# Five scheduling edits around the end of a recurrence: interleaving rate, page pool, load order, integer positions, gate rank

## The chip, the cores and the metric

The kernel runs on one core of one Trainium2 chip, as a single launch. The metric is the device time of that launch in microseconds; lower is better. A core has five engines with a queue of instructions each: TensorE (PE; its weight loads are shown as PEld), VectorE (DVE), ScalarE (ACT), GpSimd (POOL), and SyncE (SP), which here only issues transfers. An engine takes its instructions in the order in which they were written down at compile time and waits on semaphores for the others. SBUF is on-chip memory, PSUM the accumulator banks of PE, DRAM the memory outside.

## The reference

One layer over 1024 tokens of width 1024, cut to what the change touches:

```python
h = adaln(x, shift1, scale1)
p = h @ w_in                                  # conv columns and recurrence columns
y_conv = silu(layer_norm(causal_conv31(glu(p_conv))))
y_rw = rwkv7(p_rw)                            # state recurrence over the 1024 tokens, 8 heads of 64
y1 = concat([y_conv, y_rw]) @ w_out
x = layer_norm(ALPHA * x + gate1 * y1)
h2 = adaln(x, shift2, scale2)
q = (h2 @ peer_wq)                            # 8 heads, two halves of 128
s1, s2 = q_first_half @ k1.T, q_second_half @ k2.T      # 128 scores each
v1, i1 = top_k(s1, 16); v2, i2 = top_k(s2, 16)
sc, ci = top_k(all 16 * 16 sums, 16)          # ci // 16 and ci % 16 are places in i1 and i2
experts, gates = i1[ci // 16] * 128 + i2[ci % 16], softmax(sc)
y2 = sum over chosen experts of gate * gelu(h2 . u[expert]) * v[expert]
x = layer_norm(ALPHA * x + gate2 * y2)
```

There are 128 * 128 experts; each token chooses 16 in each of 8 heads.

## The kernel before

The tokens are eight tiles of 128, worked in four pairs of 256 (PB) for the part after the recurrence.

**First stage, to about 240 us.** The first half of the tokens goes through `inproj(0)`: norm, projection by `proj` (24 matmuls to a weight tile, one `yield` after each), and the inputs of the recurrence, written to DRAM.

**Recurrence, about 240 to 1012 us.** 16 chunks of 64 tokens. `solve(c)` prepares a chunk without the state and runs two chunks ahead (`flight`); `pass_state(c)` carries the state through; `group_norm` finishes every second chunk. These are chains of small matmuls with DVE and ACT steps between. Into them goes other work: each group of small matmuls ends in a call of `fill()`, which adds `rate[0]` to a credit and, at a credit of RUN = 4, takes four steps of the generators in `side`. A step is the code from one `yield` to the next, mostly one matmul of a projection. `rate[0]` is RATES[0] = 1.0 while `side` holds `inproj(1)` and becomes RATES[1] at the end of chunk 3. At the end of chunks 3, 7 and 11 a `front` (output projection and norms of a pair) is appended to `side`; at 3 and 7 also a `query` (query projection, scores, choice). Before chunk 5 what is left of `inproj(1)` is drained, before chunk 9 what is left of the first front and query. `fill()` also advances `slow` (convolutions and choices) at every fourth call, and `gates` at every twelfth.

**After the recurrence, to about 1445 us.** `side` gets the last `front` (pair 768), `query(512)` and `query(768)`. A loop steps `side`, `slow` at every second turn and `gates` at every twelfth (TGATE). The last front takes its pages from a pool of its own, pg2, with NP2 = 20 pages of 2 KB a partition on the right side of SBUF. Everything else takes pages from pgp, which has NPAGE = 31.

**The choice.** `query` ends by appending one `choose` per tile to `slow`. For each head, DVE forms 72 candidate sums (`cand`, L904), and `best16` (L767 to L771) finds the best 16 values (`top`) and their positions (`pos`, uint32). L912 is an ACT copy of the positions to f32 (`fp`). L913 to L915 compare them with 32, 48 and 64; L917 to L930 work out with shifts the two places in i1 and i2. L935 copies the indices, L940 builds a one-hot tensor on DVE, and POOL multiplies and sums it (L943 to L951). L954 to L960 are the softmax on `top`, with the exponential L956 on ACT. The results go to DRAM as `sel_d` (L932). Tiles 5, 6 and 7 (GT) are later served by gathering expert rows; for 6 and 7 the choice is made in the expert stage by `choose_late`, two heads at a time, through the same function.

**The gates.** For tiles 0 to 4 (DT) `gate_matrix` reloads `sel_d` (L973), transposes it on PE (L979), and builds, four tokens at a time, the dense gate of each token over all experts: DVE L991 and L995, POOL L997, ACT L1000 and L1001, four matmuls L1003, ACT copy L1004. 32 such steps make a tile; the result goes to DRAM as `G_d`.

**Experts, about 1445 us to the end.** For tiles 0 to 4 all experts are computed densely, in 32 groups: `mg` (L1227) multiplies the expert rows with h2, kept on chip as `h2h` and `h2l` (a value and its remainder, 8 tiles of 128x640 each). They are loaded at L1080 from DRAM into a pool that takes the place of pg2. ACT applies Gelu, DVE the gate, `md` (L1261) the second matrix. Beside it run the gathers of tiles 5 to 7 on POOL and DVE.

**Order.** The compiler's scheduler plans the whole program on a timeline of its own and writes down one fixed order for each engine. Among the instructions that are ready by that timeline it takes the one traced first; a pool's slot is handed out when its earlier tile has been released. `tc.issue_after(ins)` puts instructions behind `ins` on the same engine's queue. `tc.high_priority(offset=n)` ranks what it encloses as if it had been traced n instructions earlier.

**Weights.** `load_split` loads a weight tile of 1 MB (already split into value and remainder when it was used before) on SP's queue into one of WSPLIT = 3 slots (L170).

Of the kernel before, what the change touches and what calls it, by code (L numbers as in the profile page):

```python
# [10 lines left out]
F32 = mybir.dt.float32  # L11
F32R = mybir.dt.float32r
BF = mybir.dt.bfloat16
I32 = mybir.dt.int32
U32 = mybir.dt.uint32
AF = mybir.ActivationFunctionType
OP = mybir.AluOpType
# [4 lines left out]
S = 1024  # L22
D = 1024
KD = 8
CW = 512
KS = 31
NH = 8
# [13 lines left out]
PB = 256  # L41
# [13 lines left out]
WRAW = 2  # L55
WSPLIT = 3
RUN = 4
NP2 = 20
PIN = 3
STEPS = 4, 3  # L60
RATES = 1.0, 0.5
NPAGE = 31
TSLOW = 2
TGATE = 12
# [16 lines left out]
def layer_kernel(ctx, tc, x, cols, c_row, cond_w, w_in, w2a2, g2, w_out, ln_rows, wq, keys, peer_u, peer_ut, peer_v, peer_vt, out):  # L81
# [39 lines left out]
    h2t_d = dram.tile([2, KD, 128, ND], F32, name="h2t_d")  # L121
    sel_d = dt([3, 128, 128], "sel_d", 8)
    score_d = {t: [dram.tile([128, 512], F32, name=f"score_d{t}_{g}") for g in range(4)] for t in range(6, 8)}
    split_d = {}

    GPART = [(0, ND // TB - 4), (ND // TB - 4, ND // TB - 1), (ND // TB - 1, ND // TB)]
    G_d = [dram.tile([32, 128, b - a, 4 * TB], F32, name=f"G_d{a}") for a, b in GPART]
# [28 lines left out]
    def page(name, dt=F32, w=512):  # L156
        return pgp.tile([128, max(w, 512)], dt, tag="pg", name=name)[:, :w]
# [6 lines left out]
    def load_split(src, j):  # L164

        both = ws.tile([128, 2, KD, 128], F32R, name="wsplit", bufs=WSPLIT)
        hi, lo = both[:, 0], both[:, 1]
        key = src.tensor.name, j
        if key in split_d:
            ld(both.bitcast(F32), split_d[key])  # L170
        else:
            raw = load_raw(src[j])
            A.activation(hi, raw, AF.Copy)  # L173
            G.tensor_sub(lo, raw, hi.bitcast(F32))  # L174
            split_d[key] = dram.tile([128, 2, KD, 128], F32, name=f"split_{key[0]}{j}")
            ld(split_d[key], both.bitcast(F32))
        return hi, lo
# [414 lines left out]
            fn(hi_, q)  # L592
            fill()

    kept, ys, late, normed = {}, {}, [], {}

    def quad(name, bufs=3):
        return rw.tile([128, 4, 64], F32, name=name, bufs=bufs)
# [174 lines left out]
    def front(t0, pg_):  # L773

        n, nt, tile0 = PB, PB // 128, t0 // 128
        fetch = [tile0 + t in GT for t in range(nt)]
        hp, hi = duo("ychi", F32R, pg_)
        lp, lo = duo("yclo", F32R, pg_)
        for i in range(KD // 2):
            f = pg_("ycf").rearrange("p (a t) -> p a t", a=2)  # L780
            if i < 2:
                c = t0 % HALF
                ld(f, conv_d[t0 // HALF][2 * i:2 * i + 2, :, c:c + n].rearrange("g p t -> p g t"))
            else:
                for t in range(nt):
                    ld(f[:, :, 128 * t:128 * t + 128],
                       rwkv_d[tile0 + t][2 * i - 4:2 * i - 2].rearrange("g p t -> p g t"))
            A.activation(hp[i], f, AF.Copy)
            G.tensor_sub(lp[i], f, hp[i].bitcast(F32))
        yield  # L790
        y1 = duo("y1", F32, pg_)[1]
        for j in range(KD):
            w = load_split(w_out, j)
            pt = mm(n)
            yield from proj(w, (hi, lo), pt)
            A.activation(y1[j], pt, AF.Copy, scale=mod[:, 16 + j:17 + j])
        rows = {}
        for nm, src in (("g1", ln_rows[0]), ("b1", ln_rows[1])) + (
                (("sh2", mod_d[3]), ("sc2", mod_d[4])) if any(fetch) else ()):
            rows[nm] = [pg_("row_" + nm) for _ in range(2)]  # L800
            s_ = src.rearrange("a b -> (a b)") if len(src.shape) == 2 else src
            for i in range(2):
                ld(rows[nm][i], s_[512 * i:512 * i + 512][None, :].to_broadcast([128, 512]))
        xn = []
        for t in range(nt):
            xt = load_x(tile0 + t, pg_)
            for i in range(2):
                pt = mm()
                for k in range(4):
                    T.transpose(pt[:, 128 * k:128 * k + 128], y1[4 * i + k][:, 128 * t:128 * t + 128], ident)  # L810
                V.scalar_tensor_tensor(xt[i], xt[i], ALPHA, pt, op0=OP.mult, op1=OP.add)
            normalize(xt, xt)
            for i in range(2):
                V.tensor_mul(xt[i], xt[i], rows["g1"][i])
                G.tensor_add(xt[i], xt[i], rows["b1"][i])
                ld(x1_d[tile0 + t][:, 512 * i:512 * i + 512], xt[i])
            xs = [pg_("xn2") for _ in range(2)]
            normalize(xs, xt)
            if fetch[t]:
                for i in range(2):  # L820
                    V.scalar_tensor_tensor(xt[i], rows["sc2"][i], 1.0, xs[i], op0=OP.add, op1=OP.mult)
                    G.tensor_add(xt[i], xt[i], rows["sh2"][i])
                    ld(h2_d[tile0 + t][:, 512 * i:512 * i + 512], xt[i])
            xn.append(xs)
            yield
        normed[t0] = xn

    def query(t0):

        n, nt, tile0 = PB, PB // 128, t0 // 128  # L830
        fetch = [tile0 + t in GT for t in range(nt)]
        xn = normed.pop(t0)
        hi, lo = duo("h2hi", F32R)[1], duo("h2lo", F32R)[1]

        def keep(k, h, l):
            for w, f in enumerate((h, l)):
                for t in range(nt):
                    if not fetch[t]:
                        d = 128 * DT.index(tile0 + t)
                        ld(h2t_d[w, k, :, d:d + 128], f[:, 128 * t:128 * t + 128].bitcast(F32))  # L840

        to_channels(xn, lambda k: mod[:, 24 + k:25 + k], lambda k: modp[:, k, 1:2], hi, lo, keep)
        yield
        vi = [page("vi").rearrange("p (q h a r) -> p q h a r", q=2, h=NH, a=2) for t in range(nt)
              if tile0 + t not in score_d]
        val = [t[:, 0] for t in vi]
        idx = [t[:, 1].bitcast(U32) for t in vi]
        for g in range(4):
            kt = pgp.tile([128, 4, 128], F32, tag="pg", name="keys")
            ld(kt, keys[:, 4 * g:4 * g + 4, :])  # L850
            qt = []
            for m in range(4):
                w = load_split(wq, 4 * g + m)
                pt = mm(n)
                yield from proj(w, (hi, lo), pt)
                if m % 2 == 0:
                    qp = page("qt").rearrange("p (a t) -> p a t", a=2)
                A.activation(qp[:, m % 2, :], pt, AF.Copy)
                qt.append(qp[:, m % 2, :])
            for t in range(nt):  # L860
                ps = mm()
                for m in range(4):
                    T.matmul(ps[:, 128 * m:128 * m + 128], qt[m][:, 128 * t:128 * t + 128], kt[:, m, :],
                             start=True, stop=True)
                s = page("s12")
                A.activation(s, ps, AF.Copy)
                if tile0 + t in score_d:
                    ld(score_d[tile0 + t][g], s)
                    yield
                    continue  # L870
                for m in range(4):
                    best16(val[t][:, 2 * g + m // 2, m % 2], idx[t][:, 2 * g + m // 2, m % 2], s[:, 128 * m:128 * m + 128])
                    yield
        for t in range(len(vi)):
            slow.append(choose(tile0 + t, val[t], idx[t], 0, NH, 4, lambda nm, d, w: page(nm, d, w), G))

    def choose_late(tt, lt):

# [10 lines left out]
    def choose(tt, val, idx, h0, nh, nb, new, E):  # L889
# [2 lines left out]
        sh3 = [128, nh, TOPK]  # L892
        quad = lambda nm, dt=F32: new(nm, dt, 4 * n).rearrange("p (q h r) -> p q h r", q=4, h=nh)
        qf, qg, qu = quad("tkf"), quad("tkg"), quad("tku", U32)
        fp, m1, m2, m3 = (qf[:, i] for i in range(4))
        top, shf, fo = qg[:, 0], qg[:, 1], (qg[:, 2], qg[:, 3])
        pos = qu[:, 0]
        shi, qi_, ri_ = (qu[:, i].bitcast(I32) for i in (1, 2, 3))
# [10 lines left out]
                best16(top[:, h], pos[:, h], cand[:, h - hh, :])  # L909
                yield  # L910

        A.activation(fp, pos, AF.Copy)  # L912
        V.tensor_scalar(m1, fp, 32.0, None, op0=OP.is_ge)  # L913
        V.tensor_scalar(m2, fp, 48.0, None, op0=OP.is_ge)
        V.tensor_scalar(m3, fp, 64.0, None, op0=OP.is_ge)  # L915
        yield
        V.tensor_add(shf, m1, m2)  # L917
        V.scalar_tensor_tensor(shf, m3, 2.0, shf, op0=OP.mult, op1=OP.add)
# [8 lines left out]
        qb = new("tkb", BF, 8 * n).rearrange("p (q h r) -> p q h r", q=8, h=nh)  # L927
        isel, jsel = qb[:, 0], qb[:, 1]
        V.scalar_tensor_tensor(isel, m1, -2.0, qi_, op0=OP.mult, op1=OP.add)
        V.tensor_sub(jsel, fp, ri_)  # L930
        yield
        put = lambda w, t: ld(sel_d[tt][w][:, h0 * TOPK:h0 * TOPK + n], t.rearrange("p h r -> p (h r)"))  # L932
        for half, sel in ((0, isel), (1, jsel)):
# [125 lines left out]
    selbank[:] = [selx.enter_context(tc.tile_pool(name="pss", bufs=1, space=PSUM, side="right")), psum]  # L1059
    pg2x = ExitStack()  # L1060
    pg2 = pg2x.enter_context(tc.tile_pool(name="pg2", bufs=NP2, side="right"))

    def page2(name, dt=F32, w=512):
        return pg2.tile([128, max(w, 512)], dt, tag="pg2", name=name)[:, :w]

    side += [front(S - PB, page2), query(S - 2 * PB), query(S - PB)]
    while side or slow or gates:
        step(side)
        fills[0] += 1
        if fills[0] % TSLOW == 0 or not side:  # L1070
            slow_step(1)
        if fills[0] % TGATE == 0 or not side:
            step(gates)

    pg2x.close()
    dp = ctx.enter_context(tc.tile_pool(name="dp", bufs=1, side="right"))
    h2h, h2l = ([dp.tile([128, ND], F32R, name=f"h2{w}{k}") for k in range(KD)] for w in "hl")
    for k in range(KD):
        for w, h in enumerate((h2h, h2l)):
            ld(h[k].bitcast(F32), h2t_d[w, k])  # L1080
    selx.close()
    fex.close()
    dl = ctx.enter_context(tc.tile_pool(name="dl", bufs=1))
# [246 lines left out]
```

## Time and profile before

| what | us |
|---|---|
| median of 3 runs | 3269.81 |
| lowest, highest | 3268.62, 3273.45 |
| the profiled execution's own time | 3266.04 |
| its span, first to last instruction | 3264.3 |
| mean granted clock of TensorE | 0.946 |

The profile is one execution. Times in it are in microseconds from the span's start. A row of a timeline gives start, length, engine, line, operation, output and inputs, and in brackets how long the engine had been idle and what released it. A row of waits gives the waiting engine and line, the releaser, the sum, the number of times and the longest. The granted clock is 1.0 at full speed and 0.5 at half.

### The profile page before, as it was taken

The page shows a single profiled execution, that of the slowest core. Times are in us where ns is not written, and L with a number is a line of the kernel's source. Part 1 is how long each engine was busy: PE and PEld are TensorE (multiplying, and loading weights), DVE is VectorE, ACT ScalarE, POOL GpSimd, SP SyncE. Part 2 cuts the span into 40 slices and gives each one's busy share as a digit, 9 for nine tenths or more (in the row PEclk, how much of TensorE's full clock was granted, in tenths as well). Part 3 has the DMA queues.
Part 4 walks back from the last instruction along what each step waited for, and adds up shares of the span by engine and source line. Part 5 has one row for each costly group of instructions (what it writes and reads, how often), then busy time and mean ns, then how long its engine had stood idle before and what let it go on. Part 6 is the DMA issues. An engine that isn't in the chain of part 4 may idle for free.

```text
span 3264.3 us, 54847 instructions
## 1 busy us (share of the span) xinstructions
PE 3033.4 (93%) x20400; PEld 2641.4 (81%) x20400; DVE 2524.4 (77%) x5588; ACT 1206.7 (37%) x2358; POOL 1822.8 (56%) x1448
## 2 busy tenths in 40 slices
PE   6968999999888689699999999999999999999995
PEld 4735667688778679698988998888999999999995
DVE  6379566747778878658999998998778777777878
ACT  5562453343255476272323232232322232222322
POOL 2410112224433654458777877677777778787872
PEclk9979899979779899799999999999999999999998
DMA  8876464458449689879998989899999999999994
GB/s 307 293 213 225 136 192 138 138 192 295 148 149 309 228 268 323 286 238 365 320 348 311 350 317 329 301 324 355 328 353 328 346 328 349 334 344 336 337 342 180
DMA packets 412364, 922.25 MB, mean 283 GB/s; under 512 B 81808, under 2 KB 222400, under 8 KB 390080
## 3 DMA queue, kind: packets, MB, share of 16 engines
q1 hardware_dynamic: 219264, 474.10, 42.0%
q0 software_dynamic: 110592, 402.70, 33.6%
q10 hardware_dynamic: 82240, 41.94, 4.6%
q8 instruction: 160, 2.62, 0.3%
q14 instruction: 108, 0.88, 0.1%
HBM read 788.58 MB, written 130.05 MB: 281 GB/s over the span
## 4 chain that ended last, share of the span: by engine, by line
PE 39%; DVE 12%; issue 5%; DMA 3%; POOL 2%; ACT 1%; ACTq 0%; POOLq 0%; DVEq 0%
PE mg L1227 18%; PE md L1261 18%; DVE grow L1153 2%; PE mm L186 2%; DVE gy L1160 2%; PE mgate L1003 1%; DVE yacc L1266 1%; POOL grow L1145 1%; DMA vraw<-peer_vt 1%; DMA grow<-peer_v,eid 1%; POOL vlo L1188 1%; DMA grow<-peer_u,eid 1%; POOL ulo L1188 1%; DMA G_d<-stage 0%; DVE mg L1231 0%
## 5 line engine op out<-in xcount | busy, mean ns | idle before, releaser
L1227 PE MATMUL mg<-h2h,uhi 128*128 128x320 f32 x2024 | 626.9, 310 | 8.7 <-DVE al L1233 8.7
L1227 PE MATMUL mg<-h2l,uhi 128*128 128x320 f32 x2024 | 625.7, 309 | 0.0
L1227 PE MATMUL mg<-h2h,ulo 128*128 128x320 f32 x2024 | 625.5, 309 | 0.0
L1160 DVE SCALAR_TENSOR_TENSOR gy<-grow,gz,gy 128x1024 f32<-128x1024 f32 x381 | 488.0, 1281 | 16.8 <-DMA grow<-peer_v,eid 12.0
L1261 PE MATMUL md<-vhi,al 128*128 128x512 f32 x1280 | 498.1, 390 | 0.3 <-DVE al L1233 0.3
L1261 PE MATMUL md<-vlo,ah 128*128 128x512 f32 x1280 | 496.9, 390 | 0.0
L1261 PE MATMUL md<-vhi,ah 128*128 128x512 f32 x1280 | 492.5, 391 | 4.2 <-ACT ah L1232 3.1
L1153 DVE SCALAR_TENSOR_TENSOR grow<-grow,gh 128x1024 f32<-128x1024 f32 x384 | 460.7, 1212 | 39.1 <-DMA grow<-peer_u,eid 34.6
L1145 POOL DMA_INDIRECT grow<-peer_u,eid x384 | 364.7, 950 | 192.9 <-DVE grow L1153 73.6
L1145 POOL DMA_INDIRECT grow<-peer_v,eid x384 | 363.3, 946 | 182.4 <-DVE gy L1160 81.5
L1227 PEld LDWEIGHTS mg<-h2h,uhi 128*128 128x128 f32 x2024 | 380.4, 188 | 17.3 <-DVE al L1233 12.6
L1227 PEld LDWEIGHTS mg<-h2l,uhi 128*128 128x128 f32 x2024 | 380.5, 188 | 5.0
L1227 PEld LDWEIGHTS mg<-h2h,ulo 128*128 128x128 f32 x2024 | 380.5, 188 | 3.1
L1188 POOL TENSOR_TENSOR ulo<-uraw,uhi 128x1024 fp32r<-128x1024 f32 x128 | 309.4, 2417 | 31.0 <-ACT uhi L1186 23.3
L1188 POOL TENSOR_TENSOR vlo<-vraw,vhi 128x1024 fp32r<-128x1024 f32 x128 | 309.5, 2418 | 25.1 <-ACT vhi L1186 22.3
L1266 DVE TENSOR_TENSOR yacc<-md,yacc 128x512 f32<-128x512 f32 x310 | 211.0, 685 | 109.0 <-PE md L1261 102.2
L1261 PEld LDWEIGHTS md<-vhi,ah 128*128 128x128 f32 x1280 | 239.5, 188 | 53.6 <-ACT ah L1232 6.4
L1261 PEld LDWEIGHTS md<-vlo,ah 128*128 128x128 f32 x1280 | 240.3, 188 | 48.8
L1261 PEld LDWEIGHTS md<-vhi,al 128*128 128x128 f32 x1280 | 240.3, 188 | 45.4 <-DVE al L1233 0.5
L1186 ACT ACTIVATE vhi<-vraw 128x1024 fp32r<-128x1024 f32 x128 | 135.2, 1056 | 380.7 <-DMA vraw<-peer_vt 324.4
L174 POOL TENSOR_TENSOR wsplit<-wraw,wsplit 128x1024 fp32r<-128x1024 f32 x46 | 113.0, 2458 | 255.7 <-ACT wsplit L173 249.7
L997 POOL TENSOR_TENSOR ob<-ob,selt 128x384 f32<-128x384 f32 x160 | 136.5, 857 | 209.4 <-DVE ob L995 142.3
(404 smaller groups left out, 6092.2 us busy)
## 6 DMA issues: line engine op xcount, KB each, us to landing
uraw<-peer_ut SPq DMA_DIRECT2D x128, 512.0 KB
vraw<-peer_vt SPq DMA_DIRECT2D x128, 512.0 KB
wsplit<-split_wq SPq DMA_DIRECT2D x48, 1024.0 KB
G_d<-stage ACTq DMA_DIRECT2D x20, 2048.0 KB
gmat<-G_d SPq DMA_DIRECT2D x32, 1024.0 KB
cw<-cond_w SPq DMA_DIRECT2D x48, 512.0 KB
wsplit<-split_w_out SPq DMA_DIRECT2D x24, 1024.0 KB
split_w_in<-wsplit SPq DMA_DIRECT2D x22, 1024.0 KB
```

Source lines behind the costliest of these rows:

```text
L174: G.tensor_sub(lo, raw, hi.bitcast(F32))
L186: T.matmul(pt, l[:, k, :], r[k], start=i == 0, stop=i == 3 * KD - 1)
L997: G.tensor_mul(ob[:, :3], ob[:, :3], gt[:, ts.start:ts.start + 3, None].to_broadcast([128, 3, 128]))
L1003: T.matmul(pt[:, t, :], ob[:, t, :], oa[:, t, :], start=True, stop=True)
L1145: G.indirect_dma_start(out=r, out_offset=None, in_=peer_u if k < 128 else peer_v, in_offset=bass.IndirectOffsetOnAxis(ap=eid[:, k % 128:k ...
L1153: V.scalar_tensor_tensor(r, r, 1.0, ht, op0=OP.mult, op1=OP.mult, accum_out=z[:, i:i + 1])
L1160: V.scalar_tensor_tensor(y, r, z[:, i - 128:i - 127], y, op0=OP.mult, op1=OP.add)
L1186: A.activation(hi, raw, AF.Copy)
L1188: G.tensor_sub(lo, raw, hi.bitcast(F32))
L1227: T.matmul(p, l[:, k, :], r[k][:, bs], start=i == 0, stop=i == 3 * KD - 1)
L1261: T.matmul(p, l[:, ts], r[:, e % 2, :], start=e == 0 and q == 0, stop=e == 3 and q == 2)
L1266: ins = V.tensor_add(ya, p, ya)
```

## The change

Five edits in one diff.

1. RATES[1] goes from 0.5 to 1.0: from chunk 4 on, each fill brings one step of `side`.
2. The two choices that `query(512)` appends (tiles 4 and 5) take their pages from pg2. As the query is defined earlier than the pool, the page function is kept in a list, `page2`.
3. `load_split` keeps the load instruction of each weight tile in `fetched`. The loads of `h2h` and `h2l` are put behind the load of tile 10 of `wq` as it was last fetched, which is by `query(768)`.
4. In `choose` the ACT copy of the positions is gone. The comparisons read the positions as int32, and the place in the second list is worked out from them by one DVE instruction. `choose_late` changes with it.
5. In the last loop the gate steps are traced with `high_priority(offset=500)`.

```diff
+HP = 'wq', 10
+GPRI = 500
+P2C = 1
...
-RATES = 1.0, 0.5
+RATES = 1.0, 1.0
...
-    split_d = {}
+    split_d, fetched = {}, {}
...
         if key in split_d:
-            ld(both.bitcast(F32), split_d[key])
+            fetched[key] = ld(both.bitcast(F32), split_d[key])
...
-    kept, ys, late, normed = {}, {}, [], {}
+    kept, ys, late, normed, page2 = {}, {}, [], {}, []
...
-            slow.append(choose(tile0 + t, val[t], idx[t], 0, NH, 4, lambda nm, d, w: page(nm, d, w), G))
+            slow.append(choose(tile0 + t, val[t], idx[t], 0, NH, 4, lambda nm, d, w, p=page2[0] if t0 == S - 2 * PB and P2C else page: p(nm, d, w), G))
...
-        fp, m1, m2, m3 = (qf[:, i] for i in range(4))
+        m1, m2, m3 = (qf[:, i] for i in range(3))
...
-        A.activation(fp, pos, AF.Copy)
-        V.tensor_scalar(m1, fp, 32.0, None, op0=OP.is_ge)
-        V.tensor_scalar(m2, fp, 48.0, None, op0=OP.is_ge)
-        V.tensor_scalar(m3, fp, 64.0, None, op0=OP.is_ge)
+        place = pos.bitcast(I32)
+        V.tensor_scalar(m1, place, 32.0, None, op0=OP.is_ge)
+        V.tensor_scalar(m2, place, 48.0, None, op0=OP.is_ge)
+        V.tensor_scalar(m3, place, 64.0, None, op0=OP.is_ge)
...
-        V.tensor_sub(jsel, fp, ri_)
+        V.scalar_tensor_tensor(jsel, place, 1.0, ri_, op0=OP.mult, op1=OP.subtract)
...
-    def page2(name, dt=F32, w=512):
-        return pg2.tile([128, max(w, 512)], dt, tag="pg2", name=name)[:, :w]
-
-    side += [front(S - PB, page2), query(S - 2 * PB), query(S - PB)]
+    page2.append(lambda name, dt=F32, w=512: pg2.tile([128, max(w, 512)], dt, tag="pg2", name=name)[:, :w])
+
+    side += [front(S - PB, page2[0]), query(S - 2 * PB), query(S - PB)]
...
-            step(gates)
+            with tc.high_priority(offset=GPRI) if GPRI else nullcontext():
+                step(gates)
...
-    for k in range(KD):
-        for w, h in enumerate((h2h, h2l)):
-            ld(h[k].bitcast(F32), h2t_d[w, k])
+    with tc.issue_after(fetched[HP].ins) if HP else nullcontext():
+        for k in range(KD):
+            for w, h in enumerate((h2h, h2l)):
+                ld(h[k].bitcast(F32), h2t_d[w, k])
```

## The prediction

> **What bounds the kernel now.** First the page: the span, the busy shares and the chain that ended last.
>
> ```profile
> span 3264.3 us, 54847 instructions
> PE 3033.4 (93%) x20400; PEld 2641.4 (81%) x20400; DVE 2524.4 (77%) x5588; ACT 1206.7 (37%) x2358; POOL 1822.8 (56%) x1448
> PE 39%; DVE 12%; issue 5%; DMA 3%; POOL 2%; ACT 1%; ACTq 0%; POOLq 0%; DVEq 0%
> ```
>
> TensorE is the engine to watch. An average over three stages hides where it idles, so next comes the busy time by stretch: the recurrence (240 to 1012 us), what follows until the experts start (to 1445), and the experts. Columns: stretch, length, then PE, PEld, DVE, ACT and POOL busy with instructions, granted clock, DMA share, GB/s.
>
> ```profile
> 240.00:1012.00 772.00, 729.21 (x7128) 563.86 (x7127) 544.39 (x1491) 315.90 (x688) 187.44 (x148) 0.88 0.56 183
> 1012.00:1445.00 433.00, 348.46 (x2671) 336.04 (x2670) 329.28 (x1149) 239.50 (x572) 222.52 (x237) 0.91 0.82 276
> 1445.00:3245.00 1800.00, 1771.27 (x9914) 1610.80 (x9912) 1504.17 (x2666) 509.92 (x847) 1346.73 (x1024) 1.00 0.91 330
> ...
> 680.00:1012.00 332.00, 304.55 (x3292) 271.24 (x3289) 235.12 (x896) 138.92 (x310) 121.16 (x104) 0.80 0.59 196
> ...
> 1040.00:1160.00 120.00, 85.05 (x612) 81.75 (x613) 96.22 (x336) 58.81 (x137) 75.53 (x82) 0.84 0.75 246
> 1320.00:1360.00 40.00, 16.41 (x98) 16.05 (x97) 38.41 (x186) 5.38 (x15) 18.07 (x14) 0.66 0.65 247
> 1360.00:1445.00 85.00, 81.79 (x652) 79.22 (x651) 37.37 (x66) 49.79 (x121) 47.40 (x60) 1.00 0.75 251
> ```
>
> The expert stage keeps PE busy for 1771 of 1800 us at full clock. Nothing in the change reaches its matmuls, so it only shifts. The stage between is where time lies: 433 - 348 = 85 us of idle PE, of which 35 in 1040 to 1160 and 23.6 in 1320 to 1360. The recurrence from chunk 9 on (680 to 1012) has 27 us of idle and a mean clock of 0.80.
>
> Third, who PE waited for between 1000 and 1450 us (engine and line, releaser, us in total, times, longest).
>
> ```profile
> ACT tkf L912 <- DVE tku L771: 53.8, 3, 22.7
> DVE oa L991 <- ACT selneg L985: 30.9, 2, 30.6
> PE mm L186 <- ACT y L796: 14.9, 4, 10.8
> PE mm L186 <- DMA wsplit<-split_wq: 14.1, 2, 12.2
> PE mm L863 <- ACT qt L858: 11.4, 1, 11.4
> ```
>
> Two of the three waits of PE come from ACT, and ACT itself stood 53.8 us at L912, the copy of the positions, behind the DVE's search. The timeline shows how one becomes the other.
>
> ```profile
> 1104.64 0.47 ACT L796 ACTIVATE y<-mm,mod 128x256 f32<-128x256 f32 x1 [3.98 <-PE mm L186]
> 1123.15 0.31 ACT L912 ACTIVATE tkf<-tku 128x128 f32<-128x128 uint32 x1 [18.03 <-DVE tku L771]
> ...
> 1123.76 0.29 ACT L956 ACTIVATE tkg<-tkg 128x128 f32<-128x128 f32 x1
> 1123.96 1.18 ACT L796 ACTIVATE y<-mm,mod 128x256 f32<-128x256 f32 x3
> ...
> 1124.46 0.58 PE L186 MATMUL mm<-ychi,wsplit 128*128 128x256 f32 x1 [10.83 <-ACT y L796]
> ...
> 1354.16 0.31 ACT L912 ACTIVATE tkf<-tku 128x128 f32<-128x128 uint32 x1 [22.73 <-DVE tku L771]
> ...
> 1354.78 0.29 ACT L956 ACTIVATE tkg<-tkg 128x128 f32<-128x128 f32 x1
> 1354.98 0.36 ACT L858 ACTIVATE qt<-mm 128x256 f32<-128x256 f32 x1
> ```
>
> ACT reached L912 too early and held three copies of y that would have freed PSUM banks; PE stood 10.8 us. At 1354 the same wait held a copy of qt. Note the row between: the exponential L956 comes right after L912, ahead of the held copies.
>
> **The change part by part.**
>
> *Positions stay integers.* Six plain and eight late choices each lose one copy on ACT, 0.31 and 0.23 us by their rows; 6 x 0.31 + 8 x 0.23 = 3.7 us of ACT, which is 37% busy: nothing by itself. The comparisons read int32 instead of f32.
>
> ```profile
> 1328.28 0.29 DVE L955 TENSOR_TENSOR tkg<-tkg,mx 128x128 f32<-128x128 f32 x1
> 1328.62 0.23 DVE L913 TENSOR_SCALAR tkf<-tkf 128x128 f32<-128x128 f32 x1
> 1332.17 0.29 DVE L922 TENSOR_TENSOR tku<-tku 128x128 int32<-128x128 int32 x1
> 1332.59 0.28 DVE L930 TENSOR_TENSOR tkb<-tkf,tku 128x128 bf16<-128x128 f32 x1
> ...
> ACT ltkg L956 <- DVE ltkg L955: 24.4, 4, 12.4
> ```
>
> L922 takes two int32 inputs at the price of the f32 form L930, so I take zero for the new operands; the bounds are -0.05 and +0.06 us (0.29 less 0.23) for three operations in 14 choices, under 3 us either way and mostly under expert matmuls. What matters is ACT's order. Without L912 the next that can hold it is L956, which waits for L955, and L955 started at 1328.28, the very time at which L912 did. So the removal alone shifts the release by under a microsecond, and in the expert stage L956 already stands 24.4 us in four late choices. The stall goes only if the planner puts the held copies ahead of L956. [...]
>
> *Activations load late.* The 16 loads of h2h and h2l leave their place and go behind the load of weight tile 10 in the last query. (The row of 1325 to 1335 counts only instructions on wsplit: PE, PEld, ACT, POOL, then clock, DMA share, GB/s.)
>
> ```profile
> h2h<-h2t_d SPq DMA_DIRECT2D x8, 320.0 KB
> 1313.03 0.32 SPq L1080 DMA_DIRECT2D h2h<-h2t_d  x1
> ...
> 1327.77 0.32 SPq L1080 DMA_DIRECT2D h2l<-h2t_d  x1
> 1328.64 1.97 SPq L170 DMA_DIRECT2D wsplit<-split_wq  x3
> ...
> 1325.00:1335.00 10.00, 0.00 (x0) 0.00 (x0) 0.00 (x0) 0.00 (x0) 0.71 1.04 401
> 1408.26 0.39 PE L1227 MATMUL md<-h2h,uhi 128*128 128x320 f32 x1
> ```
>
> They are 16 x 320 KB = 5.2 MB, 13 us at the 401 GB/s of that stretch, and three weight loads stood behind them: PE's 12.2 us wait. Their first use is 1408 us, so there is room. Yet PE then met the qt wait until 1355, which the search ends; removing only the first wait lengthens the second. Of the 23.6 us of idle I take a third, 8; bounds 0 and 23.6. [...]
>
> *Third choices in the last pair's pages.* Tiles 4 and 5 take pages of the 20-page pool of the last front instead of the 31 shared ones. No instruction changes. It removes page waits of the last query, which no row shows, and it lets h2h, which takes that pool's space, be loaded only when both choices are written out. That ends at 1382.5 now (the last put of sel_d), 26 us ahead of the first use; minus 13 for the load leaves 13. Zero, bounds -8 to +13.
>
> *Late gates forward.* In the last loop a gate step ranks 500 instructions earlier. The last gate matrix starts after 30.6 us in which DVE stood for ACT at L985, behind POOL's sums and the round trip through DRAM; rank can't shorten that. From 1360 on PE is 82 of 85 us busy. Zero; bounds as the 3 us of idle there, either way.
>
> *One step for each step.* From chunk 4 each fill advances the other work by one step, not half. A chunk has 64 + 16 + 4 = 84 fills (solve, pass, norm). Solves stop two chunks ahead, so chunks 9 to 15 hold some 500 fills: 250 more steps stand ahead of the recurrence's end.
>
> ```profile
> 1356.62 13.01 PE mm L186 x96
> L750 PE MATMUL bank<-eye,yt x256: 218/218/366, 427.3 to 1011.4; 64*64 64x64 f32 x128
> ```
>
> At 13.01/96 = 0.136 us a step they are 34 us of PE, and now stand behind 1011 us. They go into a stretch with 27 us of idle and clock 0.80. If all fits, 34 us are won; if the recurrence ends 34 us later, nothing; if besides the later stage cannot shrink, 34 are lost. I take half, 17: idle and clock leave room, but PE is 92% busy there. The second query also ends nearer to the recurrence, so tiles 2 and 3 choose some 34 us earlier, partly off the third front: of the 14.9 us for y I take 5.
>
> **Sum:** 17 + 5 + 8 = 30 us. The profiled execution took 3266.04 (span 3264.3 and 1.7 around it); 3236 for it. The median of the runs, 3269.81, lies 3.8 above it: **3240**.
>
> **The rivals.**
>
> *The waits swap places* (no change to slightly faster). L956 holds ACT where L912 did, h2h's loads come back as contention, and the recurrence ends later by what it took in. For: the L956 rows; the PE share of 92%. Against: the whole order is planned anew. It gives 0 to 12 us less: 3258 to 3270.
>
> *The holes fill too* (faster). The copies do get ahead of L956 and more weight is ready at the recurrence's end: all 14.9 + 23.6 and the 34: 72 us less, 3197; with only part of it, 3195 to 3222. For: 85 us of idle PE. Against: L955's times.
>
> *The recurrence becomes the long pole* (slower). Its matmuls queue behind 250 more steps, it ends 34 us later, and what follows (last front, norms, choice of tile 4, gates) is a chain of waits that keeps its 433 us with less to fill it. It decides from where the later stage shrinks less than the recurrence grows. Price: 3266 + 34 - 8 = 3292, with the 3.8: 3296; half of it 3279. For: the waits above are of latency, not of work. Against: two queries still fill that stage.
>
> **How the numbers follow.** Forecast 0.46 (its own range 3222 to 3258), holes fill too 0.18, waits swap 0.16, long pole 0.20. What a measurement tells from no change is about 0.2%, 6.5 us. Of the swap, 0.12 lies within and 0.04 beyond it: faster 0.68, same 0.12, slower 0.20. The range reaches into both outer cases, leaving some 0.08 below 3203 and 0.11 above 3288.
>
> **What would show it.** Right: the rows of 1320 to 1360 with less than 15 us of idle PE, no wait of PE on split_wq beside h2h, mg at most 30 us earlier than 1441, last L750 below 1030. Wrong: L956 at 18 and 23 us in ACT's waits (integers bought nothing); L750 beyond 1040 with a later stage still over 420 us (the long pole); SP standing at L1080 with weight loads behind it (pages held too long); an expert stage that isn't 1800 us.

## The result and the profile after

| | before | changed |
|---|---|---|
| median, us | 3269.22 (4 runs, 3262.59 to 3273.45) | 3229.15 (4 runs, 3222.70 to 3243.18) |
| the profiled execution: span, us | 3264.3 | 3220.9 |
| its mean granted clock | 0.946 | 0.959 |

The ratio of the changed kernel to the one before is 0.9886, with a 95% interval of 0.9855 to 0.9918: 1.1% faster, about 40 us, where 30 were forecast. One of the 12 executions of `int_rate` (below) took 3772 us at a granted clock of 0.736; its ratio leaves that one out, its median doesn't.

The page of the changed kernel, with the span, the busy shares and the chain that ended last:

```profile
span 3220.9 us, 54828 instructions
PE 3009.8 (93%) x20400; PEld 2618.9 (81%) x20400; DVE 2524.3 (78%) x5588; ACT 1199.7 (37%) x2342; POOL 1825.0 (57%) x1448
PE 42%; DVE 14%; DMA 6%; issue 3%; POOL 2%; ACT 2%; ACTq 0%; POOLq 0%; DVEq 0%; SPq 0%
```

DVE, ACT and POOL do the same amount of work as before to within 7 us. PE shows 24 us less busy time (3033.4 before) with the same 20400 matmuls, at a higher mean clock (0.959, before 0.946). So the change didn't take work away. It moved it.

Two landmarks tell how far. The first row is of the last small matmuls of the recurrence, the second of the first product of the experts, both of the changed kernel (instructions, shortest/median/longest ns, first to last start); the third is the second one's counterpart of before.

```profile
L753 PE MATMUL bank<-eye,yt x256: 217/219/367, 420.8 to 1030.9; 64*64 64x64 f32 x128
L1230 PE MATMUL mg<-h2h,uhi x2024: 302/309/469, 1398.2 to 3160.7; 128*128 128x320 f32 x184
```

```profile
L1227 PE MATMUL mg<-h2h,uhi x2024: 302/309/636, 1441.2 to 3204.0; 128*128 128x320 f32 x184
```

From the first mg to the last it took 1762.8 us before and 1762.5 after: the expert stage only shifted, by 43.0 us. The recurrence ends 19.5 us later (1011.4 before). What follows it, up to the first mg, shrank from 429.8 to 367.3 us, by 62.5, and the difference is the gain.

The stretches of the prediction, changed kernel, the experts' moved by their 43 us (length, busy us of PE, PEld, DVE, ACT and POOL, granted clock, DMA share, GB/s):

```profile
240.00:1012.00 772.00, 731.01 (x7290) 567.41 (x7289) 562.63 (x1571) 318.61 (x698) 192.53 (x152) 0.92 0.58 193
...
1402.00:3202.00 1800.00, 1771.61 (x9914) 1612.60 (x9912) 1504.53 (x2668) 507.92 (x840) 1344.30 (x1024) 0.99 0.91 330
1320.00:1360.00 40.00, 34.38 (x272) 33.65 (x273) 10.62 (x25) 12.11 (x31) 25.09 (x33) 0.96 0.93 338
680.00:1012.00 332.00, 315.52 (x3575) 282.73 (x3573) 251.59 (x984) 144.68 (x329) 122.77 (x106) 0.89 0.64 217
```

In 680 to 1012 PE did 283 more matmuls than before (3575 against 3292) at a clock of 0.89 instead of 0.80. In 1320 to 1360, where PE had stood 23.6 of 40 us, it stands 5.6. But that is other work: VectorE, 38.41 us of 40 busy there before with the searches of the last two choices, is busy 10.62 now, as these are over by 1320. The same searches now fill 1285 to 1325, and there PE stands 7.0 us:

```profile
1285.00:1325.00 40.00, 33.01 (x242) 31.99 (x243) 38.79 (x200) 12.60 (x32) 19.69 (x14) 0.91 0.75 255
```

Last the waits that the prediction began with (engine and line, releaser, us in total, times, longest), 1000 to 1450 us, changed kernel:

```profile
ACT tkg L959 <- DVE tkg L958: 28.7, 3, 16.2
...
PE mm L189 <- ACT y L799: 10.1, 2, 9.6
```

ACT's 53.8 us at the copy are gone, but 28.7 us at the exponential have come in their place. The timeline of the second pair of choices shows what is behind it (start, length; in brackets the idle time before and its releaser):

```profile
1072.70 0.31 ACT L959 ACTIVATE tkg<-tkg 128x128 f32<-128x128 f32 x1 [16.17 <-DVE tkg L958]
...
1075.51 1.18 ACT L799 ACTIVATE y<-mm,mod 128x256 f32<-128x256 f32 x3
```

```profile
1076.02 0.58 PE L189 MATMUL mm<-ychi,wsplit 128*128 128x256 f32 x1 [9.56 <-ACT y L799]
```

ACT stands 16.17 us at the exponential, the copies of y come after it, and PE stands 9.56 us for them. That is the same picture as before, with another instruction at its head, and it isn't this wait that the change removed. At the last pair of choices the picture is another: PE had waited 12.2 us for weights and 11.4 for a copy of qt, and now no wait of either kind is over 2.2 (1290 to 1400 us).

```profile
PE mm L189 <- DMA wsplit<-split_wq: 4.4, 4, 1.4
...
PE mm L866 <- ACT qt L861: 2.2, 1, 2.2
```

Which edits did what, the experiments have to say.

### The profile page after: what moved, and what is told of

Same layout as the page of the kernel before. It is cut to its first block, busy times and chain, and to the rows that moved or that the text cites. A ratio compares the mean times of both kernels' runs of the same rounds, so it can differ in the third digit from the quotient of the medians.

```text
span 3220.9 us, 54828 instructions
## 1 busy us (share of the span) xinstructions
PE 3009.8 (93%) x20400; PEld 2618.9 (81%) x20400; DVE 2524.3 (78%) x5588; ACT 1199.7 (37%) x2342; POOL 1825.0 (57%) x1448
## 4 chain that ended last, share of the span: by engine, by line
PE 42%; DVE 14%; DMA 6%; issue 3%; POOL 2%; ACT 2%; ACTq 0%; POOLq 0%; DVEq 0%; SPq 0%
PE mg L1230 19%; PE md L1264 19%; DVE grow L1156 3%; PE mm L189 2%; DMA G_d<-stage 2%; DVE yacc L1269 1%; PE mgate L1006 1%; DVE gy L1163 1%; DMA grow<-peer_u,eid 1%; DMA vraw<-peer_vt 1%; DMA grow<-peer_v,eid 1%; DMA wsplit<-split_wq 1%; POOL vlo L1191 0%; DVE cand L907 0%; POOL ulo L1191 0%
## 5 line engine op out<-in xcount | busy, mean ns | idle before, releaser
L1163 DVE SCALAR_TENSOR_TENSOR gy<-grow,gz,gy 128x1024 f32<-128x1024 f32 x381 | 488.0, 1281 | 17.0 <-DMA grow<-peer_v,eid 14.9
L1230 PEld LDWEIGHTS mg<-h2h,uhi 128*128 128x128 f32 x2024 | 380.7, 188 | 14.8 <-DVE al L1236 10.2
L1191 POOL TENSOR_TENSOR vlo<-vraw,vhi 128x1024 fp32r<-128x1024 f32 x128 | 309.2, 2416 | 24.9 <-ACT vhi L1189 22.6
```

What stands on the lines that cost most here:

```text
L1163: V.scalar_tensor_tensor(y, r, z[:, i - 128:i - 127], y, op0=OP.mult, op1=OP.add)
L1230: T.matmul(p, l[:, k, :], r[k][:, bs], start=i == 0, stop=i == 3 * KD - 1)
```

## The experiments

All of them compute the whole layer. Each is the kernel before or the changed one with single edits in or out; the ratio is to the kernel before on the same chip, with its 95% interval.

### The rate alone, and all but the rate

```diff
-RATES = 1.0, 0.5
+RATES = 1.0, 1.0
```

`only_rate` is this edit alone.

> Before plus RATES 1.0 alone. Theory (the rate carries the gain: the second query ends at the recurrence's end instead of 48 us behind it, so the third and last fronts start earlier): 3225 to 3245 us, last second-query matmul near 1010 us, last recurrence transpose near 1030 us. Rival (the freed ACT queue and the late loads carry it): 3260 to 3275 us. Rival (chance of the planner's order; no edit has an effect of its own): anywhere from 3240 to 3285 us, with landmarks that differ from those of the whole change.

`no_rate` is the changed kernel without it.

> The whole change without the rate (RATES 0.5). Theory of the rate: 3255 to 3270 us, the second query ends near 1045 us again. Rival (ACT and loads): 3230 to 3245 us.

Measured: `only_rate` 3275.04 us, ratio 1.0022 [1.0003, 1.0040]; `no_rate` 3233.25 us, 0.9895 [0.9870, 0.9920]. So the rate alone costs some 7 us, and the changed kernel can do without it. The first row is of `only_rate`, the second of `no_int` (below), both of the end of the recurrence:

```profile
L753 PE MATMUL bank<-eye,yt x256: 218/218/367, 420.8 to 1062.4; 64*64 64x64 f32 x128
```

```profile
L753 PE MATMUL bank<-eye,yt x256: 218/218/367, 426.5 to 1067.5; 64*64 64x64 f32 x128
```

Alone, the rate moves the end of the recurrence from 1011.4 to 1062.4 us, 51 us, more than the 34 us of steps that it moves in. That is the rival of the long pole, though what follows doesn't keep its length as the rival had it: it gets shorter by 46, less than the 51. In the changed kernel the end is at 1030.9.

A difference of some 10 us in such a landmark tells nothing by itself, since each kernel has one trace: in `only_hp` (below) VectorE runs its 5588 instructions in the very sequence of before, and its recurrence ends 9.6 us earlier.

```profile
L753 PE MATMUL bank<-eye,yt x256: 218/218/366, 421.9 to 1001.8; 64*64 64x64 f32 x128
```

### The integers alone, and all but the integers

```diff
-        fp, m1, m2, m3 = (qf[:, i] for i in range(4))
+        m1, m2, m3 = (qf[:, i] for i in range(3))
...
-        A.activation(fp, pos, AF.Copy)
-        V.tensor_scalar(m1, fp, 32.0, None, op0=OP.is_ge)
...
+        place = pos.bitcast(I32)
+        V.tensor_scalar(m1, place, 32.0, None, op0=OP.is_ge)
...
-        V.tensor_sub(jsel, fp, ri_)
+        V.scalar_tensor_tensor(jsel, place, 1.0, ri_, op0=OP.mult, op1=OP.subtract)
```

> Before plus integer positions alone. Theory: ACT stands at the exponential for as long as at the copy (18, 13 and 23 us before), because the exponential waits for the same search; 3263 to 3272 us. Rival (the copy was what held ACT): the three waits of 54 us in sum fall below 20 us, and the time to 3240 to 3255 us.

> The whole change with the positions copied by ACT again. If the integers' 15 us of the run alone add to the rest: 3240 to 3250 us. If the exponential holds ACT for as long anyway and the 15 us came from another order: 3225 to 3237 us.

Measured: `only_int` 3253.29 us, 0.9952 [0.9930, 0.9973]; `no_int` 3269.50 us, 1.0009 [0.9993, 1.0024]. Alone the edit brings 0.48%, 15.7 us of 3268. Taken out of the changed kernel, it takes the whole gain with it. This is the edit that I had put at zero.

It doesn't win its time at the last pair of choices, where the prediction looked. There ScalarE stands 22.8 us at the exponential, as it had at the copy, and PE's two waits are as before (`only_int`, 1290 to 1400 us):

```profile
ACT tkg L959 <- DVE tkg L958: 32.2, 2, 22.8
...
PE mm L189 <- DMA wsplit<-split_wq: 14.5, 2, 12.9
PE mm L866 <- ACT qt L861: 10.6, 1, 10.6
```

At the end of the second pair `only_int` is already 10.0 us ahead of before (second exponential at 1113.8 and 1123.8 us), at the first mg 11.4. Of that it has 4.3 at the first exponential of all, ahead of which VectorE and ScalarE run the same instructions in both.

### Pages, loads and gates alone

`only_p2c` has P2C = 1 and the page list, `only_hp` the order of the h2h and h2l loads, `only_gpri` the gates' rank, each alone; `no_gpri` is the changed kernel with GPRI = 0.

> Before plus the third choices' pages alone. Theory G: 3262 to 3275 us; without the late loads the 16 loads of h2h and h2l must now wait for the choices, and weight loads may stand behind them. Rival P (pages of the last query free sooner): 3240 to 3258 us.

> Before plus the late load of h2h and h2l alone. Theory: PE's 12 us wait for weights at 1325 to 1337 us goes, but PE then stands longer for the copy of qt, which the choice releases at 1355 us; 3260 to 3270 us. Rival (the loads' place was worth its 12 us): 3253 to 3259 us.

> Before plus the gates' rank alone. After the rate and the late loads gave nothing by themselves (1.002 and 1.000) and the integers 0.995, theory G (the gates' rank carries most of the rest: gate steps of tiles 2 to 4 fill the time of the last front and its norms, so less of them is left for the queries): 3235 to 3255 us, and the last gate matmul 15 to 30 us ahead of 1444 us. Rival P (the pages carry it): 3262 to 3273 us here.

> The whole change without the gates' rank. Theory G: 3245 to 3262 us, most of the gain goes. Rival P: 3225 to 3240 us. Rival (the edits make up for one another): within 5 us of the whole change, as it was without the rate.

Measured: `only_p2c` 3256.39 us, 0.9971 [0.9951, 0.9991]; `only_hp` 3267.89, 0.9997 [0.9978, 1.0015]; `only_gpri` 3264.41, 0.9992 [0.9976, 1.0008]; `no_gpri` 3235.34, 0.9912 [0.9882, 0.9943]. The pages bring some 9 us alone, the loads and the gates nothing that can be measured.

The loads show a wait that another takes the place of. PE's waits from 1290 to 1400 us in `only_hp`:

```profile
PE mm L189 <- ACT s L869: 14.9, 1, 14.9
PE mm L189 <- DMA wsplit<-split_wq: 7.8, 2, 5.6
```

The weights' longest wait fell from 12.2 to 5.6 us, and PE met 14.9 us for a copy of scores instead. The timeline of the same kernel says why ACT made it late: it stood 17.67 us at the copy of positions, for VectorE's search.

```profile
1344.13 0.31 ACT L915 ACTIVATE tkf<-tku 128x128 f32<-128x128 uint32 x1 [17.67 <-DVE tku L774]
```

```profile
1345.57 0.58 PE L189 MATMUL mm<-h2hi,wsplit 128*128 128x256 f32 x1 [14.88 <-ACT s L869]
```

With the pages alone the loads of h2h and h2l are issued from 1381 us on instead of 1313 (the pool that h2h takes over is still held by the choices until then). The weights aren't behind them either, and here the wait for qt shrinks too (`only_p2c`, 1290 to 1400 us):

```profile
PE mm L189 <- DMA wsplit<-split_wq: 9.3, 5, 3.5
PE mm L866 <- ACT qt L861: 4.1, 1, 4.1
```

PE gets 14 us more done in 1320 to 1360 (row of `only_p2c`; before: 16.41):

```profile
1320.00:1360.00 40.00, 30.58 (x228) 29.86 (x227) 37.79 (x159) 8.39 (x22) 20.45 (x16) 0.91 0.63 228
```

### What in the integers does it: the copy on ScalarE, or the operands of VectorE

`copy_act` is the changed kernel with the copy on ScalarE put back and read by nobody:

```diff
-        m1, m2, m3 = (qf[:, i] for i in range(3))
+        m1, m2, m3, fp = (qf[:, i] for i in range(4))
...
+        A.activation(fp, pos, AF.Copy)
         place = pos.bitcast(I32)
```

> The changed kernel with one instruction put back in each choice: ScalarE copies the positions to floats again, and nothing reads the copy; the comparisons and the subtraction stay on the integers. Theory 1 (ScalarE, in order, stands at the copy until the search ends and holds the recurrence's and the front's copies behind it): most of the gain is lost, 3255 to 3275 us, the last transpose of the recurrence after 1050 us (1030.9 changed, 1067.5 without integers), and ScalarE's wait at the copy at least 20 us between 680 and 1070 us. Theory 2 (VectorE no longer waits for ScalarE between the search and the one-hots, and its one-hots get ahead of GpSimd's multiplications, 882 ns mean against 1261 ns without integers): the gain stays, 3225 to 3238 us, with one-hots below 1000 ns. Theory 3 (only the planner's order, which any edit shifts): no pattern, anything from 3229 to 3275.

`copy_dve` has float positions again, but VectorE makes the copy:

```diff
-        m1, m2, m3 = (qf[:, i] for i in range(3))
+        m1, m2, m3, fp = (qf[:, i] for i in range(4))
...
-        place = pos.bitcast(I32)
+        V.tensor_copy(fp, pos)
+        place = fp
...
-        V.scalar_tensor_tensor(jsel, place, 1.0, ri_, op0=OP.mult, op1=OP.subtract)
+        V.tensor_sub(jsel, fp, ri_)
```

> The changed kernel with float positions, but the copy to floats made by VectorE itself, right after its search, instead of ScalarE. Theory 1 (ScalarE held): the gain stays, 3228 to 3240 us; the 14 copies of 0.2 to 0.3 us cost under 4 us. Theory 2 (no hand-over between the engines): the same, 3228 to 3240. If the integer operands themselves were what helps: 3260 to 3275.

Measured: `copy_act` 3239.34 us, 0.9918 [0.9903, 0.9933]; `copy_dve` 3268.14 us, 1.0001 [0.9989, 1.0013]. Theory 1 falls on both sides. With the copy back on ScalarE most of the gain stays, though ScalarE stands 46.7 us at it (680 to 1450 us; 12.2 of them before 1070, where the theory wanted 20):

```profile
ACT tkf L915 <- DVE tku L774: 46.7, 6, 15.3
```

And with no copy on ScalarE at all, but floats on VectorE, nothing of the gain is left. Theory 2 is right about `copy_act`, 1.3 us beyond its range, and wrong about `copy_dve`: the hand-over between the engines isn't it either. The two kernels differ in what VectorE reads, in the copy that it makes, and in the order that the scheduler plans from it.

The trace shows one difference where VectorE goes on, at the one-hot tensors. The timeline of before, in the last pair of choices (DVE first, then POOL, which multiplies each one-hot as it is done), and the one-hots' row by tile with shortest/median/longest ns:

```profile
1332.79 5.92 DVE L940 TENSOR_TENSOR oh<-iota_q,tkb 128x1024 bf16<-128x1024 bf16 x4
1338.64 6.04 DVE L904 TENSOR_TENSOR cand<-vi 128x128 f32<-128x128 f32 x4
...
1333.62 2.23 POOL L943 TENSOR_TENSOR oh<-oh,tkb 128x1024 bf16<-128x1024 bf16 x1 [28.34 <-DVE oh L940]
```

```profile
L940 DVE TENSOR_TENSOR oh<-iota_q,tkb x4: 685/1540/2399, 1332.8 to 1336.3; 128x1024 bf16<-128x1024 bf16 x4
```

and the same place in the changed kernel:

```profile
1300.57 2.50 DVE L943 TENSOR_TENSOR oh<-iota_q,tkb 128x1024 bf16<-128x1024 bf16 x4
1302.98 2.41 DVE L907 TENSOR_TENSOR cand<-vi 128x128 f32<-128x128 f32 x4
...
1301.39 3.95 POOL L946 TENSOR_TENSOR oh<-oh,tkb 128x1024 bf16<-128x1024 bf16 x1 [18.23 <-issue]
```

```profile
L943 DVE TENSOR_TENSOR oh<-iota_q,tkb x4: 687/689/690, 1300.6 to 1302.4; 128x1024 bf16<-128x1024 bf16 x4
```

The same four one-hots take 5.92 us in one and 2.50 us in the other, the four sums for the next search 6.04 and 2.41. The instructions are the same in form, and in this stretch in order. In both kernels the first multiplication of GpSimd starts 0.8 us after the first one-hot. Before, it takes 2.23 us, and VectorE's one-hots are up to 2.40 us long; after, it takes 3.95 us, and all four of VectorE's are 0.69. In these rows the instructions of one of the two engines are long beside the other's; whose they are differs. The later instructions of that search give a part back, and from the first softmax of the pair to the second it is 25.9 us before (L955 at 1328.28 and 1354.17) and 20.9 after (L958 at 1298.03 and 1318.93): 5 us of VectorE's search, for which ScalarE's copies of the last query wait. The rows of before:

```profile
1328.28 0.29 DVE L955 TENSOR_TENSOR tkg<-tkg,mx 128x128 f32<-128x128 f32 x1
...
1354.17 0.29 DVE L955 TENSOR_TENSOR tkg<-tkg,mx 128x128 f32<-128x128 f32 x1
```

and of after:

```profile
1298.03 0.28 DVE L958 TENSOR_TENSOR tkg<-tkg,mx 128x128 f32<-128x128 f32 x1
...
1318.93 0.28 DVE L958 TENSOR_TENSOR tkg<-tkg,mx 128x128 f32<-128x128 f32 x1
```

The mean of the 24 one-hots tells roughly how many of them were long. Over all kernels:

| kernel | VectorE reads | copy on ScalarE | one-hot, mean ns | median us | ratio |
|---|---|---|---|---|---|
| int_p2c | integers | no | 830 | 3234.56 | 0.9910 |
| int_rate | integers | no | 861 | 3249.36 | 0.9955 |
| copy_act | integers | yes | 878 | 3239.34 | 0.9918 |
| changed | integers | no | 882 | 3229.15 | 0.9886 |
| no_gpri | integers | no | 946 | 3235.34 | 0.9912 |
| only_int | integers | no | 972 | 3253.29 | 0.9952 |
| no_rate | integers | no | 973 | 3233.25 | 0.9895 |
| only_gpri | floats | yes | 1122 | 3264.41 | 0.9992 |
| only_rate | floats | yes | 1259 | 3275.04 | 1.0022 |
| no_int | floats | yes | 1261 | 3269.50 | 1.0009 |
| before | floats | yes | 1264 | 3269.22 | 1 |
| only_hp | floats | yes | 1264 | 3267.89 | 0.9997 |
| only_p2c | floats | yes | 1265 | 3256.39 | 0.9971 |
| copy_dve | floats | no | 1291 | 3268.14 | 1.0001 |

The seven kernels with integers have the seven shortest means, and every median with integers lies below every one with floats. The nearest two, `only_int` (0.9930 to 0.9973) and `only_p2c` (0.9951 to 0.9991), can't be told apart, though. Within a group the mean doesn't order the times, so it isn't the whole price. The two group rows of the trace, before and changed (busy us and mean ns behind the bar):

```profile
L940 DVE TENSOR_TENSOR oh<-iota_q,tkb 128x1024 bf16<-128x1024 bf16 x24 | 29.1, 1264 | 0.0
```

```profile
L943 DVE TENSOR_TENSOR oh<-iota_q,tkb 128x1024 bf16<-128x1024 bf16 x24 | 19.8, 882 | 0.0
```

What stays open: the planned order changes as well. In its trace `copy_act` runs 5587 of VectorE's 5588 instructions in the sequence of the changed kernel. Of `no_int` at most 4905 can be matched to it in sequence, of `copy_dve` 5047 (what the edit itself changes counted as equal). The two ends of this pair of experiments thus differ in order and in which engine's instructions are long, and no run held one of them fixed.

Where the time goes speaks against the one-hots as the main cause. The rows are of the stretch from the second choice to the end of the recurrence, in `copy_dve` and `copy_act`, then in `only_rate` and `int_rate`, which are the integers apart:

```profile
853.00:1064.00 211.00, 182.30 (x2014) 163.83 (x2012) 159.93 (x602) 93.86 (x222) 67.04 (x71) 0.85 0.54 181
848.00:1034.00 186.00, 174.67 (x2001) 157.43 (x2002) 153.91 (x547) 90.28 (x218) 65.69 (x71) 0.90 0.58 188
...
850.00:1062.00 212.00, 189.52 (x1973) 168.66 (x1974) 156.78 (x585) 91.21 (x219) 66.14 (x71) 0.81 0.54 175
846.00:1031.00 185.00, 174.16 (x1998) 156.77 (x1998) 152.58 (x541) 90.18 (x216) 65.74 (x71) 0.90 0.58 188
```

In both couples PE runs the same matmuls to within 2%, with floats in 25 and 27 us more: it stands 17 and 12 us longer, and its matmuls take 8 and 15 us more at a lower granted clock (0.85 against 0.90 and 0.81 against 0.90). Only four one-hots fall into the stretch, and with floats they are 0.6 us longer in sum; VectorE's whole busy time is 6 and 4 us longer. So most of what the two couples differ by (29 and 26 us in the medians) comes up where hardly a one-hot runs. The planned order is the nearest rival for it, and no run tested it. In the kernels with the rate at 0.5 the recurrence ends at about the same time with integers and with floats (1001 to 1014 us), and the gain comes up behind it.

In its last pair `copy_dve` has short one-hots too, a median of 685 ns (the row below, 1290 to 1375 us), and is slow nevertheless: its recurrence ends at 1063.8 us, and what follows is late.

```profile
L944 DVE TENSOR_TENSOR oh<-iota_q,tkb x8: 684/685/2403, 1341.1 to 1365.7; 128x1024 bf16<-128x1024 bf16 x8
```

And `only_int` has a one-hot of 2.40 us in its last pair, so integer operands don't always keep VectorE's one-hots short. What does wasn't tried.

### Integers with the pages, integers with the rate

`int_p2c` is the kernel before with the integers and the pages; `int_rate` the kernel before with the integers and the rate.

> The kernel before with integer positions and the third choices in the last pair's pages, nothing else. If the two gains that each has alone add up (1 - 0.9952 and 1 - 0.9971 of 3268): about 3243 us, and what is left to 3229 is the rate's, the loads' and the gates' with them. If they meet the same wait: 3250 to 3257, as the integers alone. If they open the way for each other as in the run without the rate: 3230 to 3237.

> The kernel before with integer positions and one step of other work for each step of the recurrence, nothing else. If the rate gives its part once the copy is gone (last transpose of the recurrence at about 1031 us as in the changed kernel, second query 15 us earlier): 3235 to 3245 us. If the rate is worth nothing and the pages are what the integers need: 3250 to 3258.

Measured: `int_p2c` 3234.56 us, 0.9910 [0.9892, 0.9927]; `int_rate` 3249.36 us, 0.9955 [0.9935, 0.9976]. The rate adds nothing to the integers (0.9952 alone). The pages add 0.42%, 14 us, to them, against 0.29% alone; 0.48 and 0.29 make 0.77, measured are 0.90, and the intervals are too wide to tell a sum from a little more than one. What is left to the changed kernel's 0.9886 is inside the intervals as well. So the change is, as far as the runs can tell, its integers and its pages.

`only_p2c` and `int_p2c` are one edit apart and show where the time comes from. Starts of the exponential, the mark of a choice, in the three pairs, with the ends of the stages on PE:

| us | only_p2c | int_p2c | earlier by |
|---|---|---|---|
| first pair of choices | 829.5, 859.4 | 824.0, 852.7 | 5.5, 6.6 |
| recurrence ends | 1012.5 | 1004.8 | 7.7 |
| second pair | 1100.5, 1125.0 | 1081.8, 1102.4 | 18.7, 22.6 |
| last front's matmuls end | 1180.3 | 1162.3 | 18.0 |
| third pair | 1327.9, 1352.5 | 1302.6, 1323.2 | 25.3, 29.3 |
| first mg | 1432.3 | 1401.4 | 30.9 |

Of these 30.9 us, 5.5 are there at the first exponential, and up to that choice VectorE and ScalarE run the same order in both kernels: most likely scatter. The second and the third pair are 3.9 us shorter each (24.5 to 20.6); there `int_p2c` has no long one-hot and `only_p2c` several of 2.40 us, and this is what the shorter one-hots give directly. The first pair, with long one-hots in both, is 1.1 us shorter. The other 16 us come up between the pairs and behind them, 12 of them between the first and the second, the stretch in which the recurrence ends and the second query and the last front share the engines. That they are due to the earlier choices is an argument from the sequence, not shown.

## Why the prediction was right in its number and wrong in its reasons

The time lies 11 us below the forecast and within the forecast's own range; the terms do not stand.

- **The bound.** That the expert stage only shifts and that the time lies between recurrence and experts was right: 1762.8 and 1762.5 us, and 62.5 us out of the stretch between.
- **"One step for each step", 17 us.** This term failed. The step was "If all fits, 34 us are won", of which I took half. Alone it costs 7 us, on top of the integers it gives nothing, and without it the changed kernel keeps its gain (3233.25 and 3229.15 us, intervals that overlap). The third rival described it better: alone, the recurrence ended 51 us later and what follows gave back 46.
- **"Positions stay integers", zero, bounds of 3 us.** This is the step that failed most. The edit was priced by ScalarE's order and by the duration of the changed instructions. The first part came true: the exponential took the copy's place and held ScalarE 16.17 us and PE 9.56 us. I took that as the sign that the integers bought nothing. They are worth 15.7 us alone, and without them the gain is gone. How they do it isn't shown. With them change the order of the whole plan and, at the one-hots, whether VectorE's instructions or GpSimd's are long, and the sum had a term for neither. A row that could have warned me of the second stood in the trace: one-hots of 0.69 and of 2.40 us in one group, which the mean of 1264 ns hides. It is worth some 4 us in a pair of choices, so it is the smaller part.
- **y, 5 us.** PE's waits for y fell from 14.9 to 10.1 us, by 4.8, but not for the reason given, the second query's earlier end by the rate. Without the rate they are 10.2 (row of `no_rate`, 1000 to 1450 us), so the size came out by luck.

```profile
PE mm L189 <- ACT y L799: 10.2, 4, 5.2
```

- **Loads late, 8 us, and pages, zero with bounds -8 to +13.** The weights' wait did go (14.1 us before; 4.4 in 1290 to 1400 us after, no single one over 1.4). But the load order alone brought nothing, for the reason that the prediction gives itself: "removing only the first wait lengthens the second". The pages, alone 9 us and with the integers 14, did the work that I had credited to the loads: with them alone the loads come later, as the prediction says under them, and both waits of PE shrink (12.2 to 3.5 us, 11.4 to 4.1). Why the copy of qt comes sooner isn't shown. So 8 us was near, under the wrong name.
- **Gates forward, zero.** Nothing that can be measured, alone or left out (0.9912 against 0.9886, the intervals overlap).
- **The rivals.** "The waits swap places" is what `only_hp` and ScalarE's exponential show, each in its place, yet not for the sum. "The holes fill too" came true at the last pair, where PE's idle went from 23.6 to 7.0 of 40 us, but not at y. Of the signs named, under 15 us of idle in 1320 to 1360 was met (5.6, of other work), the last L750 "below 1030" missed by 0.9, and mg came 43.0 us earlier, more than the "at most 30".

The sum was right because a term of 17 that isn't there stood in for one of zero that is. That is luck.

## What to carry to other kernels

An edit of a few instructions in a program that is planned as a whole changes the order everywhere, so a price from the edited instructions and their neighbours on one engine isn't enough. Afterwards, compare kernels that are one edit apart by a few landmarks (here the end of the recurrence at 1031 or 1062 us), and find out first how far these scatter between traces of one order. Look at the shortest and longest of a group of equal instructions, not only at the mean: the group here that ran at 0.69 and at 2.40 us had a partner on another engine, whose lengths changed too (1.91 to 3.95 us). With several edits in one change, taking each out of the whole answers another question than putting each in alone: the integers were 0.5% alone and all of the gain at the end, and the rate, to which the forecast gave most, was worth nothing in company and a loss by itself. And a forecast that lands on the number has not shown its reasons.

## What the runs showed of the hardware

That instructions of VectorE and GpSimd get longer beside each other was not in my sum. At 843.76 us of the changed kernel a one-hot of 128x1024 bf16 has no work of GpSimd beside it and takes 0.69 us, and its multiplication, 1.91 us from 844.59 us on, has no one-hot beside it. Every one-hot of 2.40 us in the two traces overlaps a multiplication of 1.9 to 2.4 us, and beside one-hots of 0.69 us a multiplication takes up to 3.95 us (last pair of the changed kernel, shortest/median/longest ns):

```profile
L946 POOL TENSOR_TENSOR oh<-oh,tkb x8: 1909/1916/3953, 1301.4 to 1330.6; 128x1024 bf16<-128x1024 bf16 x8
```

The 1.71 us that a long one-hot takes more are most of a multiplication of 1.91 us, as far as GpSimd's spans can be read. Why one of the two gets long isn't shown. Which of the two will be long can't be read from the recorded starts: in both kernels the multiplication is recorded 0.4 us ahead of the third one-hot (1333.62 and 1333.99 us before, 1301.39 and 1301.78 after), and before the one-hot takes 2.40 us, while after it takes 0.69. The third one-hots of before and after:

```profile
1333.99 2.40 DVE L940 TENSOR_TENSOR oh<-iota_q,tkb 128x1024 bf16<-128x1024 bf16 x1
```

```profile
1301.78 0.69 DVE L943 TENSOR_TENSOR oh<-iota_q,tkb 128x1024 bf16<-128x1024 bf16 x1
```

What tips it isn't in these rows.

ScalarE's order, on which the prediction leaned, is borne out by `copy_act`: the engine stands 46.7 us at a copy whose result nobody reads. In the last of these waits it stands 11.75 us, and three copies of qt, which don't need the search, follow only behind the copy (1321.23 and 1322.18 us). Only it isn't what set the time there.
